# Mixture-of-experts block on one core: weight loads asked ahead in the dense stage, sliced table writes, and a fetch one chunk ahead in the second stage

## The chip, the cores and the metric

The kernel runs on one core of a Trainium2 chip. The metric is the time of one execution on the device in microseconds (us), taken as the median of several runs.

## The reference

The reference is one transformer block in fp32 on 512 tokens of width 2048: a mixer (attention and a recurrent unit, with modulated norms), then a layer of 16384 experts, then a final norm. The change touches the expert layer alone:

```python
q = (h @ w_q).reshape(B, S, 8, 2, 128)
s1 = einsum('bshd,hnd->bshn', q[..., 0, :], k1)     # 128 keys for each head
s2 = einsum('bshd,hnd->bshn', q[..., 1, :], k2)
v1, i1 = top_k(s1, 16);  v2, i2 = top_k(s2, 16)
vs, ic = top_k(v1[..., :, None] + v2[..., None, :], 16)   # best 16 of 256 sums
e = i1[ic // 16] * 128 + i2[ic % 16]                # 16 experts of 16384 a head
w = softmax(vs)
act = gelu(einsum('thkd,td->thk', u[e], h)) * w
y = einsum('thk,thkd->td', act, v[e])
```

Each token so has 128 chosen experts (8 heads, 16 each) out of 16384.

## The kernel before, in words

**How the work is split.** The 512 tokens are four tiles of 128. One tile is done by gathers: for each of its 128 choices, one row of u per token is gathered (L744), multiplied with the token and summed on DVE (L758), later one row of v is gathered and added on DVE (L756). This "side work" is sent in small portions between other work. The other three tiles (384 tokens) are done densely, in two stages.

**The dense stage** (about 1073 to 2370 us) multiplies all 16384 rows of u with the 384 tokens, as 128 blocks of 128 experts. `ublock` does a block in two halves. For each half `stream` loads 512 KB through SP's queue into `raw` (four buffers), and `hilo` splits it into two parts for precise fp32 products: a cast on ACT (L94) gives the high part, a subtraction on DVE (L95) the low part (three buffers each). Then come 24 matmuls (L690: eight column groups by three products). After each half, `pump` runs the list `todo`: 0.9 rows of side work, and one scatter of a list, if there is one. At the block's end ACT applies the gelu (L694, two buffers), and SP writes the result to two tables in memory: 128 KB to `tab2` (L696: two token tiles side by side) and 64 KB to `tab1` (L698: the third).

Between the blocks lie other pieces of work, traced in this order:
- Three decodes of the top choices (L611 to L640, on DVE), of which each ends in PE transposes (`rows`), with `ublocks(1)` to `ublocks(3)` after them. `ublocks(n)` does the blocks up to number n.
- Constants, and the zero fill of the tables' first rows and of two lists (DVE L811 and L815, writes of SP L812, L813, L817).
- `halves_of`, three times: for a token tile it builds the matrix of routing weights, 64 tokens at a time, so six "halves" in all. Sixteen steps of four tokens each make one-hot rows on DVE (L909, L914), multiply them on PE (L915, the "expansion matmuls", 768 in all) and copy the result on ACT into `ws` (L916, 4 MB, one buffer). The blocks are dealt out between the steps, 17 to a half. After the 16 steps, four writes of 1 MB go from `ws` to the table through SP's queue (L920, rows of 256 bytes), and four reductions of `ws` run on DVE (L921).
- `make_list`, twice: it picks out the rows of the table that any token uses (rounds of a maximum operation on DVE, a block after each fourth), scatters the list to memory (POOL, one to a `pump`) and reads it back (`done`, L890, on SP).
- The late top-k of the third tile: eight loads of scores (L934, `s12`, two buffers, SP), each followed by a search on DVE.

**The second stage** (about 2370 to 3104 us) goes through the listed rows in 171 chunks of 128 experts. `vchunk` gathers 128 rows of v (`gr`, L968 and what follows) and the rows of a table (`gw`), multiplies gelu and weight on DVE (L978), splits this into `gh` and `gl` (three buffers), splits the v rows in two halves (ACT L94, DVE L95), and multiplies on PE (L991), in the order gh with the high part, gh with the low part, gl with the high part. `vrun` calls `vchunk` for each chunk and then `step`, which sends the rest of the side work, and later the output's pieces. The first 76 chunks are 52 that serve two token tiles and 24 of the first tile alone; the other 95 serve one tile each and make up the stretch after about 2740 us.

**What orders the work.** The kernel is written in a language in which a planner orders each engine's instructions: program order is the priority, and an instruction whose inputs the planner expects later may be passed by a later one. `tc.keep_in_program_order(x)` takes this freedom away: x stays behind the instruction of the same engine that was traced before it. Each engine executes its own sequence in order, and a DMA is issued by one engine's queue (SP's, ACT's or POOL's) at its place in that sequence. An instruction that waits holds up all that stand behind it in that queue.

## Time and profile before

| | before |
|---|---|
| median of 3 runs | 3125.18 us (3118.3 to 3130.12) |
| the profiled execution | 3117.84 us, of which the span is 3116.0 us |
| busy PE | 2859.3 us (92%) |
| busy weight loads of PE | 2497.1 us (80%) |
| busy DVE | 2487.7 us (80%) |
| busy ACT | 1221.3 us (39%) |
| busy POOL | 928.6 us (30%) |
| bytes moved by DMA | 869.30 MB, mean 279 GB/s |
| mean granted clock of PE | 0.961 of full speed |

PE is TensorE, DVE is VectorE, ACT is ScalarE, POOL is GpSimd, SP is SyncE, which issues most of the loads and writes. "SPq" stands for SP's queue of DMA issues. A line of the profile names a line of the code (L690), the engine, the operation, and output<-input by the tiles' names; a number after x is a count; "<-" in a wait names what ended it. A matmul's weight load has rows of its own (PEld). The share of busy time over the whole span mixes three stages with different limits: the mixer and the projections up to 1073 us, the dense stage up to 2370 us, and the second stage up to 3104 us, with an end of 12 us behind it. The granted clock says at which share of its full speed PE was run.

### The profile page before, as it was taken

To read this page: it belongs to the slowest core of one execution; us is meant where nothing else is said; L and a number is where in the kernel's file an instruction comes from. 1 tells how busy PE (TensorE), PEld (TensorE's weight loads), DVE (VectorE), ACT (ScalarE), POOL (GpSimd) and SP (SyncE) were. 2 spreads that over 40 slices of the span, in tenths; PEclk is the share of its full clock that TensorE was granted. 3 is DMA by queue.
4 is the path that set the end of the run, shared out by engine and by line. 5 is a ranking of instruction groups with operands and counts; after the bars stand their busy time and mean duration, and the time that the engine had idled before them with its cause. 6 is when DMAs were issued, how large, how long until landed. Compare 5 with 4: busy or idle time off the path is not lost.

```text
span 3116.0 us, 39002 instructions
## 1 busy us (share of the span) xinstructions
PE 2859.3 (92%) x14093; PEld 2497.1 (80%) x14093; DVE 2487.7 (80%) x4100; ACT 1221.3 (39%) x1653; POOL 928.6 (30%) x673
## 2 busy tenths in 40 slices
PE   7899999989999999988899989998878999888887
PEld 5577777768788899988889989998877777766665
DVE  6877777873368898999988889999768888777777
ACT  5322223662232243333322223334223444555665
POOL 0000000000020002222223352422448777477774
PEclk9999999999999999999999999999989999999999
DMA  9767777333322368999999989999989999978885
GB/s 344 292 226 232 246 234 237 111 106 129 122 89 90 109 203 331 334 320 304 313 394 402 400 307 345 347 297 307 343 336 397 371 353 359 350 278 321 344 317 218
DMA packets 329502, 869.30 MB, mean 279 GB/s; under 512 B 125682, under 2 KB 181362, under 8 KB 274388
## 3 DMA queue, kind: packets, MB, share of 16 engines
q0 software_dynamic: 72512, 477.03, 40.5%
q1 hardware_dynamic: 256352, 389.52, 37.3%
q8 instruction: 112, 1.84, 0.2%
q14 instruction: 90, 0.74, 0.1%
q10 hardware_dynamic: 436, 0.18, 0.0%
HBM read 805.38 MB, written 61.25 MB: 278 GB/s over the span
## 4 chain that ended last, share of the span: by engine, by line
PE 56%; DVE 12%; DMA 10%; issue 7%; ACT 3%; POOL 2%; SPq 1%; another core or an unknown queue 0%; DVEq 0%; ACTq 0%; POOLq 0%
PE pj L690 25%; PE ps L991 11%; PE pj L660 6%; PE ps L526 4%; DMA araw<-w_ada 4%; DVE slo L95 4%; PE pj L302 3%; PE pj L991 2%; PE ps L915 2%; DVE gr L758 1%; DMA raw<-tab,igown 1%; PE pj L526 1%; DVE F L921 1%; ACT shi L94 1%; POOL gr L744 1%
## 5 line engine op out<-in xcount | busy, mean ns | idle before, releaser
L690 PE MATMUL pj<-dh,slo 128*128 128x384 f32 x2048 | 698.9, 343 | 53.7 <-DVE slo L95 53.5
L690 PE MATMUL pj<-dh,shi 128*128 128x384 f32 x2048 | 699.6, 342 | 21.1 <-ACT shi L94 21.1
L690 PE MATMUL pj<-dl,shi 128*128 128x384 f32 x2048 | 696.8, 340 | 0.0
L94 ACT CAST shi<-raw 128x1024 fp32r<-128x1024 f32 (+1 forms) x402 | 417.6, 1047 | 632.8 <-PE pj L690 243.5
L95 DVE TENSOR_TENSOR slo<-raw,shi 128x1024 fp32r<-128x1024 f32 (+1 forms) x402 | 487.7, 1217 | 217.1 <-ACT shi L94 196.3
L690 PEld LDWEIGHTS pj<-dh,slo 128*128 128x128 f32 x2048 | 392.4, 192 | 60.8 <-DVE slo L95 60.4
L95 DVE TENSOR_TENSOR slo<-gr,shi 128x1024 fp32r<-128x1024 f32 x342 | 405.6, 1222 | 41.4 <-ACT shi L94 34.6
L690 PEld LDWEIGHTS pj<-dh,shi 128*128 128x128 f32 x2048 | 393.3, 192 | 22.2 <-ACT shi L94 22.2
L690 PEld LDWEIGHTS pj<-dl,shi 128*128 128x128 f32 x2048 | 392.5, 192 | 0.1
L94 ACT CAST shi<-gr 128x1024 fp32r<-128x1024 f32 x342 | 342.1, 1046 | 107.6 <-PE ps L991 60.2
L744 POOL DMA_INDIRECT gr<-u_rows,ei x128 | 173.9, 1358 | 678.5 <-DVE gr L758 313.9
L756 DVE SCALAR_TENSOR_TENSOR y<-gr,dots,y 128x2048 f32<-128x2048 f32 x128 | 300.7, 2349 | 36.7 <-DMA gr<-v_rows,ei 36.4
L991 PE MATMUL ps<-shi,gh 128*128 128x512 f32 x740 | 254.0, 414 | 73.3 <-ACT gh L94 42.0
L148 DVE SCALAR_TENSOR_TENSOR araw<-araw,sil 128x1024 f32<-128x1024 f32 x192 | 233.8, 1222 | 104.8 <-DMA araw<-w_ada 101.9
L991 PE MATMUL ps<-slo,gh 128*128 128x512 f32 x740 | 297.4, 408 | 6.9 <-DVE slo L95 6.9
L758 DVE SCALAR_TENSOR_TENSOR gr<-gr,hrow 128x2048 f32<-128x2048 f32 x128 | 292.3, 2284 | 4.0 <-issue 4.0
L744 POOL DMA_INDIRECT gr<-v_rows,ei x128 | 198.3, 1549 | 311.4 <-DVE y L756 161.3
L991 PE MATMUL ps<-shi,gl 128*128 128x512 f32 x740 | 275.2, 399 | 1.6 <-DVE gl L95 1.6
L679 POOL CAST dh<-hh 128x384 fp32r<-128x384 f32 x16 | 10.4, 648 | 855.1 <-DVE hh L573 855.1
L991 PEld LDWEIGHTS ps<-shi,gh 128*128 128x128 f32 x740 | 143.9, 196 | 122.2 <-ACT gh L94 50.3
L694 ACT ACTIVATE ge<-pj 128x384 f32<-128x384 f32 x128 | 62.8, 490 | 422.4 <-PE pj L690 334.5
L302 PE MATMUL pj<-hh,shi 128*128 128x512 f32 x528 | 214.0, 405 | 6.6 <-ACT w L478 3.5
(353 smaller groups left out, 4996.2 us busy)
## 6 DMA issues: line engine op xcount, KB each, us to landing
raw<-peer_u SPq DMA_DIRECT2D x256, 512.0 KB
araw<-w_ada SPq DMA_DIRECT2D x192, 512.0 KB
raw<-w_in SPq DMA_DIRECT2D x66, 512.0 KB
tab<-ws SPq DMA_DIRECT2D x24, 1024.0 KB
raw<-w_out SPq DMA_DIRECT2D x32, 512.0 KB
raw<-w_q SPq DMA_DIRECT2D x32, 512.0 KB
tab<-ge SPq DMA_DIRECT2D x128, 128.0 KB
tab<-ge SPq DMA_DIRECT2D x128, 64.0 KB
```

The lines of the kernel that those rows point to most:

```text
L94: A.copy(hi, src)
L95: V.tensor_tensor(out=lo, in0=src, in1=hi, op=OP.subtract)
L148: V.scalar_tensor_tensor(out=r, in0=r, scalar=1.0, in1=sil[:, half * 1024:half * 1024 + 1024], op0=OP.mult, op1=OP.mult, accum_out=acc[:, ...
L302: PE.matmul(p, l[:, k8 * 128:k8 * 128 + 128], r, start=(k == 0 and i == 0), stop=(k == KC - 1 and i == 2))
L526: PE.matmul(po[t], l[:, ts], r[:, sl], start=(k == 0 and i == 0), stop=(k == KC - 1 and i == 2))
L660: PE.matmul(p, l[:, k8 * 128:k8 * 128 + 128], r, start=(k == 0 and i == 0), stop=(k == KC - 1 and i == 2))
L690: PE.matmul(p[:, :NDT], l[:, k8 * 128:k8 * 128 + 128], r, start=(k == 0 and i == 0), stop=(k == KC - 1 and i == 2))
L694: A.activation(ge, p[:, :NDT], AF.Gelu_apprx_tanh)
L744: return G.indirect_dma_start(out=out, out_offset=None, in_=src, in_offset=bass.IndirectOffsetOnAxis(ap=idx, axis=0))
L756: V.scalar_tensor_tensor(out=y0, in0=r, scalar=dots[:, j:j + 1], in1=y0, op0=OP.mult, op1=OP.add)
L758: V.scalar_tensor_tensor(out=r, in0=r, scalar=1.0, in1=hrow, op0=OP.mult, op1=OP.mult, accum_out=dots[:, j:j + 1])
L991: PE.matmul(banks[t][half * 2 + q2], l[:, ts], x[:, sl], start=first and i == 0, stop=end and i == 2)
```

## The change

It does five things:
- `uload` asks for the loads of u up to four halves ahead of their use, and keeps each in program order on SP. `ublock` takes the loaded tiles from a list.
- The two writes of a gelu result go through ACT's queue (`nc.scalar`).
- Each half's four writes of 1 MB become 32 slices of 128 KB, kept in program order on SP. They and the four reductions are put into a list, of which each `pump` takes five entries, ahead of the other work in `todo`. The blocks of a half are dealt out a little earlier, and the last of them follow after the slices were listed.
- `vchunk` is split in two: `vfetch` has the gathers, the product and the split into `gh` and `gl`; `vrun` calls it one chunk ahead.
- The order of the three products of the second stage becomes gh with the high part, gl with the high part, gh with the low part.

```diff
--- before.py
+++ after.py
@@ -680,10 +680,23 @@
             G.tensor_copy(dl[k], wl2[k][:, 128:])
     hps.close()
 
+    loads = []
+    asked = [0]
+
+    def uload(upto):
+        while asked[0] < min(upto, 2 * NB):
+            r = raw.tile([128, 1024], F32, name="raw")
+            tc.keep_in_program_order(nc.sync.dma_start(r, a["peer_u"][asked[0] // 2, asked[0] % 2]))
+            loads.append(r)
+            asked[0] += 1
+
     def ublock(b):
         p = pbank()
         for half in range(2):
-            uh, ul = stream(a["peer_u"][b, half])
+            uload(2 * b + half + 4)
+            uh = hl.tile([128, 1024], F32R, name="shi")
+            ul = hl.tile([128, 1024], F32R, name="slo")
+            hilo(uh, ul, loads.pop(0))
             for k8 in range(8):
                 k = half * 8 + k8
                 for i, (l, r) in enumerate(three(uh, ul, dh[k], dl[k])):
@@ -693,9 +706,9 @@
         ge = gq.tile([128, NDT], F32, name="ge")
         A.activation(ge, p[:, :NDT], AF.Gelu_apprx_tanh)
         rows = slice(128 + b * 128, 256 + b * 128)
-        nc.sync.dma_start(tab2[rows].rearrange("p (t x) -> p t x", t=2)[:, :, 0:128],
+        nc.scalar.dma_start(tab2[rows].rearrange("p (t x) -> p t x", t=2)[:, :, 0:128],
                           ge[:, 128:384].rearrange("p (t x) -> p t x", t=2))
-        nc.sync.dma_start(tab1[rows, 0:128], ge[:, 0:128])
+        nc.scalar.dma_start(tab1[rows, 0:128], ge[:, 0:128])
 
     dn = ExitStack()
     otp = pool(dn, "otp", side="right")
@@ -793,6 +806,14 @@
             if scatters:
                 scatters.pop(0)()
 
+    slices = []
+
+    def slices_some(n):
+        for _ in range(n):
+            if slices:
+                slices.pop(0)()
+
+    todo.append(lambda: slices_some(5))
     todo.append(lambda: side.send(GRATE))
     todo.append(lambda: scatter_some(1))
     for t in (1, 2):
@@ -902,7 +923,7 @@
             h0 = hf * TH
             ws = dz.tile([128, NB, TH], F32, name="ws")
             for t4 in range(TH // 4):
-                ublocks(lo + hf * step + t4 * (step - 3) // (TH // 4))
+                ublocks(lo + hf * step + t4 * (step - 5) // (TH // 4))
                 p = bank()
                 o1 = dz.tile([128, 4, 128], F32, name="o1", bufs=2)
                 t0 = h0 + t4 * 4
@@ -915,10 +936,19 @@
                     PE.matmul(p[:, j * 128:j * 128 + 128], o2, o1[:, j], start=True, stop=True)
                 A.copy(ws[:, :, t4 * 4:t4 * 4 + 4].rearrange("p i t -> p t i"), p.rearrange("p (t i) -> p t i", t=4))
             F = dz.tile([128, NB], F32, name="F", bufs=4)
-            for i in range(4):
-                sl = slice(i * 32, i * 32 + 32)
-                nc.sync.dma_start(tab[128 + i * 4096:4224 + i * 4096, c0 + h0:c0 + h0 + TH].rearrange("(i p) t -> p i t", p=128), ws[:, sl])
-                V.tensor_reduce(F[:, sl], ws[:, sl], axis=AX.X, op=OP.max)
+
+            def write(i, ws=ws, c=c0 + h0):
+                tc.keep_in_program_order(nc.sync.dma_start(
+                    tab[128 + i * 512:640 + i * 512, c:c + TH].rearrange("(i p) t -> p i t", p=128), ws[:, i * 4:i * 4 + 4]))
+
+            def most(i, ws=ws, F=F):
+                V.tensor_reduce(F[:, i * 32:i * 32 + 32], ws[:, i * 32:i * 32 + 32], axis=AX.X, op=OP.max)
+
+            for i in range(32):
+                slices.append(lambda i=i, w=write: w(i))
+                if i % 8 == 4:
+                    slices.append(lambda i=i // 8, m=most: m(i))
+            ublocks(lo + hf * step + step)
             Fs.append(F)
         V.tensor_tensor(out=Fs[0], in0=Fs[0], in1=Fs[1], op=OP.max)
         return Fs[0]
@@ -963,7 +993,7 @@
 
     halves = tab2.rearrange("r (h c) -> (r h) c", h=2)
 
-    def vchunk(ch, banks, flags, rows):
+    def vfetch(ch, rows):
         (idg, idv), c, top, ts_ = ch
         nt = len(ts_)
         w = nt * 128
@@ -977,6 +1007,11 @@
         g3 = gw.rearrange("p (t x) -> p t x", t=nt)
         V.tensor_tensor(out=g3[:, :, :128], in0=g3[:, :, :128], in1=g3[:, :, 128:], op=OP.mult)
         hilo(gh.rearrange("p (t x) -> p t x", t=nt), gl.rearrange("p (t x) -> p t x", t=nt), g3[:, :, :128])
+        return r, gh, gl
+
+    def vchunk(ch, got, banks, flags):
+        ts_ = ch[3]
+        r, gh, gl = got
         for half in range(2):
             pc = pieces(half)
             vh = pc.tile([128, 1024], F32R, name="shi")
@@ -987,7 +1022,7 @@
                 for j, t in enumerate(ts_):
                     first, end = flags[t]
                     ts = slice(j * 128, j * 128 + 128)
-                    for i, (l, x) in enumerate(((gh, vh), (gh, vl), (gl, vh))):
+                    for i, (l, x) in enumerate(((gh, vh), (gl, vh), (gh, vl))):
                         PE.matmul(banks[t][half * 2 + q2], l[:, ts], x[:, sl], start=first and i == 0, stop=end and i == 2)
 
     def main(n, more=False):
@@ -1012,12 +1047,15 @@
 
     def vrun(chunks, banks, both, step):
         where = {t: [i for i, ch in enumerate(chunks) if t in ch[3]] for t in range(3)}
+        ahead = []
         for i, ch in enumerate(chunks):
+            for k in range(i + len(ahead), min(i + 2, len(chunks))):
+                ahead.append(vfetch(chunks[k], gb if both(k) else vrp))
             flags = {t: (i == where[t][0], i == where[t][-1]) for t in ch[3]}
             for t in ch[3]:
                 if t not in banks:
                     banks[t] = four()
-            vchunk(ch, banks, flags, gb if both(i) else vrp)
+            vchunk(ch, ahead.pop(0), banks, flags)
             step(i)
 
     def mixed(xs, ys):
```

## Rows read from the trace of the kernel before

**Rows 1.** windows by stage: us, busy (x) per engine, PEclk, DMA share, GB/s

```profile
1073.00:2370.00 1297.00, 1203.52 (x6967) 1190.74 (x6966) 1155.50 (x1632) 429.05 (x508) 402.00 (x274) 0.96 0.93 329
1570.00:1780.00 210.00, 210.00 (x1206) 210.00 (x1206) 171.35 (x152) 61.23 (x76) 68.07 (x51) 0.99 1.02 404
2370.00:2740.00 370.00, 350.89 (x1476) 277.44 (x1475) 299.29 (x339) 173.38 (x228) 253.27 (x180) 0.98 0.95 363
2740.00:3104.00 364.00, 305.58 (x1195) 233.74 (x1193) 283.71 (x415) 221.75 (x308) 252.52 (x182) 0.94 0.81 303
```

**Rows 2.** waits of PE, 1073 to 2370: us in total, times, longest us

```profile
PE pj L690 <- DVE slo L95: 53.5, 18, 13.2
PE pj L690 <- ACT shi L94: 21.1, 5, 7.6
```

**Rows 3.** waits of SP's queue, 1190 to 2370

```profile
SPq L696 <- ACT ge L694: 358.8, 91, 8.4
```

**Rows 4.** timeline of SP at the end of the first half: start us, us, instruction

```profile
1302.24 17.63 SPq L920 DMA_DIRECT2D tab<-ws  x4
1319.97 7.29 SPq L99 DMA_DIRECT2D raw<-peer_u  x1
```

**Rows 5.** windows, sum of six, from 1300, 1380, 1460, 1540, 2090, 2160

```profile
sum 220.00, PE 167.76 PEld 160.52 DVE 195.32 ACT 63.76 POOL 35.92; mean PE 27.96 PEld 26.75 DVE 32.55 ACT 10.63 POOL 5.99
```

**Rows 6.** windows, sum of two, 1840 to 1870 and 2260 to 2300

```profile
sum 70.00, PE 43.16 PEld 41.88 DVE 40.20 ACT 9.70 POOL 34.86; mean PE 21.58 PEld 20.94 DVE 20.10 ACT 4.85 POOL 17.43
```

**Rows 7.** timeline of SP at the second list's read

```profile
2262.44 0.60 SPq L698 DMA_DIRECT2D tab<-ge  x1
2276.25 0.55 SPq L890 DMA_DIRECT2D sg<-list  x1
```

**Rows 8.** timeline of SP in the steady stretch

```profile
1588.05 0.53 SPq L696 DMA_DIRECT2D tab<-ge  x1
...
1596.42 0.52 SPq L696 DMA_DIRECT2D tab<-ge  x1
```

**Rows 9.** timeline of DVE, end of the third decode

```profile
1182.73 0.29 DVE L631 TENSOR_TENSOR se<-se,abf 128x128 f32<-128x128 f32 x1
...
1186.71 0.48 DVE L811 MEMSET pad<- 128x512 f32 x1
```

**Rows 10.** timeline of SP at the start of the dense stage

```profile
1071.26 0.38 SPq L722 DMA_DIRECT2D hrow<-hspill  x1
...
1188.31 0.88 SPq L817 DMA_DIRECT2D list<-padi  x2
```

**Rows 11.** timeline of POOL at the start of the dense stage

```profile
1180.34 0.13 POOL L808 IOTA pm<- 128x1 f32 x1 [48.86 <-DVE se L628]
```

**Rows 12.** groups of DVE, 1085 to 1187: xcount, busy us, mean ns, idle before

```profile
L95 DVE TENSOR_TENSOR slo<-raw,shi 128x1024 fp32r<-128x1024 f32 x25 | 30.4, 1219 | 4.9 <-ACT shi L94 4.9
```

**Rows 13.** timeline of SP at the late top-k

```profile
1808.51 1.24 SPq L934 DMA_DIRECT2D s<-sspill  x2
```

**Rows 14.** timeline of DVE at the late top-k

```profile
1808.61 0.28 DVE L831 TENSOR_SCALAR ig<-lf,pm 128x128 int32<-128x128 f32 x1
```

**Rows 15.** groups of DVE, 1800 to 1905

```profile
L589 DVE FIND_INDEX8 i<-v,s 128x8 uint32<-128x128 f32 x14 | 3.9, 285 | 0.0
...
L588 DVE MAX8 vs<-cd 128x8 f32<-128x256 f32 x6 | 2.5, 418 | 0.0
```

**Rows 16.** waits of PE, 2740 to 3104

```profile
PE ps L991 <- ACT gh L94: 42.0, 19, 5.1
```

**Rows 17.** timeline of DVE in the second stage

```profile
2900.38 6.94 DVE L95 TENSOR_TENSOR slo<-gr,shi 128x1024 fp32r<-128x1024 f32 x6 [0.26 <-issue]
2907.25 0.48 DVE L978 TENSOR_TENSOR raw<-raw 128x128 f32<-128x128 f32 x2
```

**Rows 18.** timeline of PE in the second stage

```profile
2907.91 0.50 PE L991 MATMUL ps<-shi,gh 128*128 128x512 f32 x1 [1.68 <-ACT gh L94]
```

**Rows 19.** waits of PE, 2370 to 2740

```profile
PE ps L991 <- ACT shi L94: 18.5, 12, 6.5
```

## The prediction

> **What bounds the kernel now.** I read the busy time by stage first. The dense stage, from 1073 to 2370 us, is 1297 us, of which PE is busy for 1203.5 us and idle for 93.5 us at a mean granted clock of 0.96 [rows 1]. One stretch of it, 1570 to 1780, shows what the stage could be: PE busy all 210 us, with DMA at its full share [rows 1]. There a half block (24 matmuls) takes 4.18 us, 1206 matmuls in 210 us, so 128 blocks need 1070 us. What is left of 1203.5 is for the 768 expansion matmuls, and for matmuls at the lower clock level. The second stage, 2370 to 3104, is 351 + 306 us of PE work and 77 us of idle time; its second part, one token tile to a chunk, is idle for 58 us of 364 [rows 1].
>
> Next, who PE waits for. In the dense stage it is the casts and differences of the weight parts (53.5 and 21.1 us) [rows 2]. Behind them lies SP's queue, which keeps its order: SP stands in front of the writes of the gelu results for 358.8 us in all, until ACT has the gelu [rows 3], and the loads that stand behind such a write wait with it. At the end of each half of the scatter-matrix work, SP is held for 17.6 us by four writes of 1 MB, and the next load takes 7.3 us more to issue [rows 4]; DVE does four reductions in a row there. The stretches around the six ends have 220 us with 167.8 us of PE work, so 52.2 us idle [rows 5]. Two others, where SP waits to read a list back before it goes on with loads, have 43.2 us of PE work in 70 us, 26.8 us idle [rows 6]: SP does nothing from 2263.0 to 2276.3 us there [rows 7].
>
> **The change, part by part.**
>
> Small writes to ACT's queue: 128 pairs leave SP, where a pair is a block apart and the first takes 0.53 us [rows 8]. ACT issues them instead, about 1.1 us more for each block of 8.36 us, in which it now has 3.4 us of work (429 us over 128 blocks [rows 1]). ACT is three parts ahead of PE; I cost this at nothing. Without that cover it would be 128 x 1.1 = 141 us. SP no longer waits for a gelu, which is the gain that the next item counts. The Trainium skill, "DMA: Bandwidth & Descriptors" (Issuing engines are not separate DMA queues), says that issuing from several engines saves only the sequencer's time for the issue. By that alone the item is worth nothing here; the row on SP's wait says that the order in the queue, not the issue, was the cost.
>
> The big writes in 32 slices, the reductions one by one, five items to a half block: 36 items take 7.2 half blocks, six times over. The 52.2 us go, but the slices ask for the same bytes within some 30 us, beside a load and 0.9 row gathers per half block, when the DMA share is already 1.02 in the steady stretch [rows 1]. Bounds: 0 (the four parts loaded ahead, 4 x 4.18 us, hide it all) and 52 us (as now). I take 18, 3 us an end, since the load now stands behind only five slices instead of four whole writes.
>
> List reads: 26.8 us now. The scatters still go one to a half block, and loads stand three half blocks ahead. I take 5 (bounds 0 and 27).
>
> Loads kept in program order: this is the part that can cost. Each load is now pinned behind the SP instruction traced before it, whatever that waits for. At the start, loads 0 to 8 are traced before the four zero-fill writes of the tables and lists; load 9 and all others stand behind them. The zero fill is written by DVE at 1186.7 us, after the last step of the third decode [rows 9], and SP issues its last writes at 1188.3 [rows 10]; until now the loads passed them. That such a thing holds up what is pinned behind it, the trace shows on POOL: its gathers wait 48.9 us for a constant in the same state [rows 11]. After the change DVE has less beside the three decodes: of the 25 differences (30.4 us) that it did between 1085 and 1187 [rows 12] only some six are left, so 22 us less, and some 5 us of waits go. The zero fill then comes near 1160, a load follows at 1162, is cast and subtracted by 1167. PE also starts late: the first loads now stand behind a read that SP issues at 1071.3 [rows 10], so PE begins near 1078 instead of 1073. It has nine half blocks, 38 us, with some matmuls of the stage before between them, until about 1119. So some 48 us of waiting and 5 us of late start: 53 us. Bounds: 0 if the fill gets memory earlier than now, 80 if the decodes go no faster.
>
> The same at the late top-k: the half loads from 151 on stand behind the last of eight reads of scores, which has two buffers, so it waits until six heads are through on DVE. In the trace the reads begin at 1808.5 us, just as DVE makes the first list's rows [rows 13, 14]. A head is ten operations of 0.28 us and six of 0.42 [rows 15], 5.3 us; six are 32 us, some 41 us with differences between. The fixed order of the list's rounds behind the blocks puts PE four parts behind, 17 us. So 24 us; bounds 0 and 41.
>
> Dense sum, idle time: 53 + 24 + 18 + 5 and 14.5 that I leave as it is (93.5 - 52.2 - 26.8) is 114.5 against 93.5, +21 us. Fewer, longer gaps let fewer matmuls run at the lower clock: 1203.5 less 1070 and about 90 for the 768 expansion matmuls and small work leaves some 43 us lost now; I take 27, -16. Together **+5 us: the dense stage gives nothing back in sum.**
>
> Second stage: in its second part PE waits 42.0 us for the cast of the gated rows [rows 16]. DVE puts the product of two gathered tiles behind six differences in a row, 6.9 us, until 2907.3 [rows 17], and PE stands 1.7 us until 2907.9 for its cast [rows 18]. With the fetch of a chunk traced ahead of the work of the one before, product and casts come first in the order, and the change of the matmuls' order asks for the second difference last. I take two thirds of the 42, 28 us, and a third of the 22 us that the clock of 0.94 over 364 us costs [rows 1], 7 us: -35. Bounds: +10 (a product waits on DVE for its gather with differences queued behind it) and -64 (58 idle and some clock; DVE has 284 us of work there, under the 300 that would leave). The waits for the weight casts in the first part, 18.5 us [rows 19], stay.
>
> **Sum:** +5 - 35 = -30 us on the profiled execution's 3117.8, 3088 us; the median of the runs is 7.3 us above that execution, so **3095 us**.
>
> **Rivals.**
>
> The pins hold nothing up (chance 0.18): the zero fill and the score reads find their memory earlier. For it: no program-order reason ties the fill to the decodes. Against: the fill follows the last decode step at once, while differences of later blocks ran before it [rows 9, 12]. Then the dense stage loses 37.5 us instead of 93.5 and 16 us of slow clock: -72 - 35, 3018 us.
>
> Slices too slow (0.20), the one that ends slower: from where five slices and a load keep SP over 4.18 us, a slice over 0.77 us. By rows, an eighth of a big write is 17.63 / 32 = 0.55 us [rows 4]; by its rows of data it has twice those of a small write of 0.53 us [rows 8], 1.06. At 1.06 SP lacks 1.45 us in each of 43 half blocks, 63 us in place of 18, and 10 us more at the low clock: 3150 us. For it: transfers already fill the DMA share. Against: 0.55 comes from the same transfer. The Trainium skill, "DMA: Bandwidth & Descriptors" (Bandwidth), has it that one should batch to 1 MiB or more, with 341 GB/s measured at 1 MB and 138 at 64 KB. By that, as an estimate, 25 MB of slices take up to 182 us instead of 74, and the change would end near 3185 us. The trace does not show it for a queue that is kept full.
>
> The order was not the cause in the second stage (0.20): the gathers themselves are late, as 0.81 of the DMA share [rows 1] makes possible, and DVE only passes it on. Then -35 goes and 3130 us is left.
>
> The forecast as worked out: 0.42.
>
> **How the numbers follow.** A measurement here can tell about 0.5%, 15.6 us. The forecast's own range is 3060 to 3135, and most of it is faster: 0.36, with 0.05 within 0.5% and 0.01 slower. The first rival adds 0.18 to faster; the second 0.20 to slower; the third 0.16 to the same and 0.04 to slower. So faster 0.54, same 0.21, slower 0.25. The range takes in the forecast, the first rival and most of the second: 3020 to 3165.
>
> **What would show it.** In the new profile: a gap of PE of some 45 us before 1170, closed by the first load after the zero fill; a second of some 20 us with SP standing before a read of scores; SP no longer waiting for the gelu; the six ends without a gap over 5 us; expansion matmuls spread over the blocks instead of bunched; PE's wait for the gated cast under 20 us after 2740. Wrong: no gap at the start (first rival), SP busy all through the slices (second), or the wait for the gated cast as long as now (third).

## The result, and the profile after

The changed kernel takes 3280.4 us (median of 6 runs) beside 3121.7 us of the kernel before: a ratio of 1.051 (95% interval 1.049 to 1.053). It is slower by 5%, where the forecast was faster by 1%. One of the six runs was in a slow state (7149 us) and is left out of the ratio. The profiled execution has a span of 3277.6 us beside 3116.0.

The stages first (busy time by stage; columns as in [rows 1], which these three lines answer). The stages' borders have moved: the last dense matmul is at 2530 us now.

```profile
1073.00:2530.00 1457.00, 1217.27 (x6951) 1194.26 (x6950) 1173.08 (x1634) 429.23 (x500) 413.85 (x275) 0.91 0.85 298
2530.00:2900.00 370.00, 344.32 (x1458) 274.21 (x1457) 279.46 (x328) 174.50 (x231) 234.01 (x175) 0.98 0.91 343
2900.00:3265.00 365.00, 314.72 (x1237) 238.67 (x1235) 288.30 (x425) 225.83 (x315) 247.71 (x186) 0.94 0.82 310
```

The whole loss lies in the dense stage: 1457 us in place of 1297. PE is idle for 239.7 us there (93.5 before), and its busy time grew by 14 us as well, with a granted clock of 0.91 in place of 0.96: after a long gap the first matmul of a half block takes 0.69 us, where one takes 0.33 in the steady stretches. From the last dense matmul to the last one of the chunks it is 734 us, 747 before.

Where the idle time lies, by stretches of the dense stage (same columns):

```profile
1119.00:1185.00 66.00, 12.31 (x53) 9.72 (x52) 56.46 (x70) 7.38 (x9) 14.34 (x14) 0.57 0.55 212
1910.00:1990.00 80.00, 47.48 (x236) 45.50 (x236) 80.00 (x185) 12.75 (x15) 17.09 (x18) 0.77 0.89 319
1990.00:2062.00 72.00, 19.10 (x97) 17.21 (x96) 72.00 (x78) 8.29 (x10) 40.62 (x20) 0.63 0.84 309
...
1460.00:1510.00 50.00, 37.38 (x193) 35.91 (x191) 28.60 (x31) 7.96 (x10) 11.27 (x9) 0.86 1.05 336
1650.00:1700.00 50.00, 33.29 (x155) 31.20 (x154) 21.80 (x20) 6.65 (x9) 8.48 (x7) 0.80 1.05 329
```

Three kinds of places can be told apart.

**The start.** PE is idle for 53.7 of the 66 us from 1119 on. PE's timeline has the gaps, SP's timeline the load that ends them:

```profile
1130.32 0.45 PE L745 MATMUL ps<-ident,se 128*128 128x128 f32 x1 [8.80 <-DVE se L628]
...
1144.58 0.48 PE L745 MATMUL ps<-ident,se 128*128 128x128 f32 x1 [13.81 <-DVE se L631]
...
1172.24 2.90 PE L936 MATMUL ps<-o,o 128*128 128x128 f32 x12 [11.53 <-DVE o L935]
...
1180.70 0.69 PE L703 MATMUL pj<-dh,shi 128*128 128x384 f32 x1 [2.08 <-ACT shi L94]
```

```profile
1081.67 14.05 SPq L689 DMA_DIRECT2D raw<-peer_u  x5
1160.81 0.33 SPq L833 DMA_DIRECT2D tab<-pad  x1
...
1163.64 1.43 SPq L689 DMA_DIRECT2D raw<-peer_u  x3
```

After nine half blocks PE goes straight to the transposes of the decodes (L745), which wait for DVE. The tenth load follows the zero fill at 1163.6 us, as the prediction had it (1162). That the fill is not what costs the time, the runs will show.

**The late top-k.** From 1910 to 2062 us PE is idle for 85.4 us. The first part is the one that was forecast: SP stands at the score reads for 31.8 us with the loads behind it. The second part was not: PE stands at the transposes of the late decode again.

```profile
1927.05 31.83 SPq L964 DMA_DIRECT2D s<-sspill  x4
```

```profile
1967.08 0.69 PE L703 MATMUL pj<-dh,shi 128*128 128x384 f32 x1 [23.48 <-ACT shi L94]
...
2025.61 0.45 PE L745 MATMUL ps<-ident,se 128*128 128x128 f32 x1 [26.22 <-DVE se L628]
...
2046.23 0.48 PE L745 MATMUL ps<-ident,se 128*128 128x128 f32 x1 [20.18 <-DVE se L631]
```

**The six ends.** Five of the six ends with slices lose 62.0 us of PE time together (the stretches from 1280, 1460, 1650, 1840 and 2160; 14.5, 12.6, 16.7, 8.0 and 10.2), and three later places lose 4.2, 7.1 and 5.6 us where the four reductions still run in a row on DVE. Before, the ends lost 52.2 [rows 5]. At the second end SP puts slices between the loads, and ACT's timeline shows who else stands:

```profile
1476.43 8.03 SPq L689 DMA_DIRECT2D raw<-peer_u  x1
1484.51 4.29 SPq L941 DMA_DIRECT2D tab<-ws  x4
...
1489.69 3.72 SPq L941 DMA_DIRECT2D tab<-ws  x5
```

```profile
1475.21 0.49 ACT L707 ACTIVATE ge<-pj 128x384 f32<-128x384 f32 x1 [0.38 <-PE pj L703]
1489.80 0.52 ACTq L709 DMA_DIRECT2D tab<-ge  x1
...
1491.13 1.04 ACT L94 CAST shi<-raw 128x1024 fp32r<-128x1024 f32 x1 [15.43 <-DMA tab<-ws]
```

The gelu is ready at 1475.7, but ACT's write of it goes out at 1489.8, and the cast that PE needs stands behind that write on ACT. Such waits, from the end of ACT's instruction before a write to the write, sum up to 133 us over the 256 small writes, 123 of it in 24 waits while slices go out.

The sixth end is different. From 2320 to 2352 us all 32 slices go out and PE does not lose anything, while POOL issues no gather (busy times of that stretch and of the second end):

```profile
2320.00:2352.00 32.00, 32.00 (x187) 32.00 (x186) 26.14 (x61) 8.69 (x11) 0.00 (x0) 1.00 1.06 260
1480.00:1512.00 32.00, 19.38 (x88) 17.91 (x87) 10.22 (x9) 4.59 (x6) 3.56 (x3) 0.79 1.04 307
```

### The profile page after: what moved, and what is told of

It reads as the page before. It is cut to its first block, busy times and chain, and to the rows that moved or that the text cites. A ratio compares the mean times of both kernels' runs of the same rounds, so it can differ in the third digit from the quotient of the medians.

```text
span 3277.6 us, 39134 instructions
## 1 busy us (share of the span) xinstructions
PE 2876.4 (88%) x14093; PEld 2502.7 (76%) x14093; DVE 2487.8 (76%) x4100; ACT 1224.3 (37%) x1652; POOL 916.3 (28%) x673
## 5 line engine op out<-in xcount | busy, mean ns | idle before, releaser
L757 POOL DMA_INDIRECT gr<-u_rows,ei x128 | 208.4, 1628 | 644.1 <-DVE gr L771 297.9
L1026 PE MATMUL ps<-shi,gh 128*128 128x512 f32 x740 | 270.3, 411 | 62.5 <-ACT gh L94 37.9
L1026 PE MATMUL ps<-shi,gl 128*128 128x512 f32 x740 | 298.8, 407 | 9.0 <-DVE gl L95 8.5
L771 DVE SCALAR_TENSOR_TENSOR gr<-gr,hrow 128x2048 f32<-128x2048 f32 x128 | 291.1, 2282 | 12.6 <-DMA gr<-u_rows,ei 12.4
L1026 PE MATMUL ps<-slo,gh 128*128 128x512 f32 x740 | 266.2, 402 | 2.3 <-DVE slo L95 2.3
L757 POOL DMA_INDIRECT gr<-v_rows,ei x128 | 179.5, 1402 | 278.8 <-DVE y L769 142.8
L302 PE MATMUL pj<-hlo,shi 128*128 128x512 f32 x528 | 213.2, 404 | 0.0
```

What stands on the lines that cost most here:

```text
L302: PE.matmul(p, l[:, k8 * 128:k8 * 128 + 128], r, start=(k == 0 and i == 0), stop=(k == KC - 1 and i == 2))
L757: return G.indirect_dma_start(out=out, out_offset=None, in_=src, in_offset=bass.IndirectOffsetOnAxis(ap=idx, axis=0))
L771: V.scalar_tensor_tensor(out=r, in0=r, scalar=1.0, in1=hrow, op0=OP.mult, op1=OP.mult, accum_out=dots[:, j:j + 1])
L1026: PE.matmul(banks[t][half * 2 + q2], l[:, ts], x[:, sl], start=first and i == 0, stop=end and i == 2)
```

## The experiments

| run | edit | median, us | ratio to before (95%) |
|---|---|---|---|
| changed kernel | | 3280.4 | 1.051 (1.049 to 1.053) |
| e2_fill | zero fill ahead of the decodes | 3282.8 | 1.054 (1.052 to 1.057) |
| e3_s12 | eight buffers for score reads | 3272.4 | 1.051 (1.048 to 1.054) |
| i2_two_pins | 2 of 256 pins left | 3271.3 | 1.047 (1.037 to 1.057) |
| i1_load_order | loads pinned to each other alone | 3186.6 | 1.020 (1.011 to 1.029) |
| e4_unpin | no load pinned | 3182.0 | 1.022 (1.019 to 1.025) |
| f1_ge_sp | e4, small writes on SP | 3172.7 | 1.018 (1.014 to 1.021) |
| h3_wide | f1, 3 entries a half block | 3165.2 | 1.016 (1.006 to 1.026) |
| g2_half | f1, 8 pieces of 512 KB | 3163.2 | 1.015 (1.011 to 1.019) |
| g1_mb | f1, 4 pieces of 1 MB | 3144.2 | 1.008 (1.005 to 1.010) |
| f3_big | e4, four writes of 1 MB at once | 3115.5 | 0.999 (0.997 to 1.000) |
| g3_big_sp | f3, small writes on SP | 3108.6 | 0.996 (0.995 to 0.998) |
| g4_pins | f3 with the pins | 3244.2 | 1.040 (1.037 to 1.043) |
| f2_ge_act | before, small writes on ACT | 3139.4 | 1.006 (1.003 to 1.009) |
| e1_second | before, second stage's part | 3106.1 | 0.997 (0.995 to 0.998) |
| f4_two | e1, two chunks ahead | 3108.0 | 0.996 (0.994 to 0.999) |
| h1_slow_slices | f1, 0.5 gathers a half block | 3250.4 | 1.043 (1.034 to 1.053) |
| h2_slow_big | g3, 0.5 gathers a half block | 3277.2 | 1.052 (1.042 to 1.062) |

Each ratio is to runs of the kernel before that were taken together with the run. The h and i runs were executed twice each, the others 4 to 12 times.

### What holds PE at the start and at the late top-k

The prediction named two holders on SP: the zero fill, and the score reads that wait for a buffer. Another was possible. What `keep_in_program_order` takes as "the instruction before" on SP need not be a DMA: where a memory pool is closed and another opened, the memory is handed over, and the planner expects that when the memory's last user is done. Behind the ninth load (load 8) the decodes' memory goes over to the pools `lp1` and `dz`; between load 156 and load 157 that of the late top-k goes over to `dz2`, and SP issues nothing else between these two. A load that is pinned there comes late in the planner's order, and with it the cast, the difference and the matmuls that use it. The hand-over is read from the program, and no trace shows it on SP. What the traces show is the order that came out of it: PE has 216 dense matmuls (9 x 24) ahead of the second decode's transposes, and 3768 (157 x 24) ahead of the late decode's. In the kernel before these counts are 376 and 4298.

The zero fill moved ahead, e2_fill:

```diff
+    with tc.tile_pool(name="tp1", bufs=1, reuse_waits="tile") as tp1:
+        pad = tp1.tile([128, 256], F32, name="pad")
+        V.memset(pad, 0.0)
+        nc.sync.dma_start(tab2[:128, :256], pad)
...
     se, wv = decode(tp, tts[0])
```

> The changed kernel with the zero fill of tables and lists written ahead of the first decode, so that no load stands behind it. Fill theory (the prediction's): the gap of PE between 1119 and 1185 us, 53 us of idle time, goes, and the time is 3225 us. Boundary theory: load 9 is pinned behind more than DMAs, namely behind the point where the memory of the third decode is handed to the next pool (pools lp1 and dz); that point waits for the decodes as well, so the gap stays and the time stays at 3280 us.

More buffers, e3_s12:

```diff
-            s12 = tp0.tile([128, 2, 128], F32, name="s12", bufs=2)
+            s12 = tp0.tile([128, 2, 128], F32, name="s12", bufs=8)
```

> The changed kernel with eight buffers in place of two for the eight score reads of the late top-k, so that no load waits for a read. Read theory (the prediction's): the loads behind the reads come 30 us earlier, the idle 86 us between 1910 and 2062 shrink to some 20, and the time is 3215 us. Boundary theory: 157 half blocks still stand ahead of the point where the late top-k's memory is handed on, which waits for its decode; PE then waits the same time in one gap in place of two, and the time is 3265 to 3280 us.

Both left the time where it was. In e2_fill the fill goes out before the first load, and SP has nothing but loads from 1072 us on. Loads 9 to 12 are issued from 1096 us on and are not held. PE still stops at the decodes' transposes after nine half blocks, and ACT's cast for the tenth comes only behind the copy of the last decode's transposes, at 1155.6 us (SP's timeline, then PE's, then ACT's):

```profile
1069.98 0.88 SPq L758 DMA_DIRECT2D list<-padi  x2
...
1072.33 126.90 SPq L689 DMA_DIRECT2D raw<-peer_u  x20
```

```profile
1096.08 11.19 SPq L689 DMA_DIRECT2D raw<-peer_u  x4
```

```profile
1138.99 0.47 PE L745 MATMUL ps<-ident,se 128*128 128x128 f32 x1 [13.68 <-DVE se L631]
```

```profile
1155.21 0.48 ACT L746 COPY oT<-ps 128x384 f32<-128x384 f32 x1 [13.08 <-PE ps L745]
1155.59 1.05 ACT L94 CAST shi<-raw 128x1024 fp32r<-128x1024 f32 x1
```

So it is not the late load but the order of PE and ACT that holds the work. The fill has a part in the gap: from 1085 to 1200 us PE is idle for 36.5 us, against 53.7. But the stage as a whole is not shorter, as other places lose more.

At the late top-k it is the same. In the changed kernel load 157 is issued at 1978.9 us, and its cast follows at 2052.4, behind the late decode (SP's timeline, then ACT's):

```profile
1978.88 80.47 SPq L689 DMA_DIRECT2D raw<-peer_u  x5
```

```profile
2046.96 0.48 ACT L746 COPY oT<-ps 128x384 f32<-128x384 f32 x1 [40.00 <-PE ps L745]
...
2052.38 2.01 ACT L94 CAST shi<-raw 128x1024 fp32r<-128x1024 f32 x2
```

In e3_s12 all score reads are out by 1891 us, the gap of 23.5 us is gone, and the wait at the decode has grown to 54.2 us from 26.2 (PE's timeline):

```profile
2019.52 0.45 PE L745 MATMUL ps<-ident,se 128*128 128x128 f32 x1 [54.16 <-DVE se L628]
...
2040.14 0.47 PE L745 MATMUL ps<-ident,se 128*128 128x128 f32 x1 [20.17 <-DVE se L631]
```

Then no pins, e4_unpin:

```diff
-            tc.keep_in_program_order(nc.sync.dma_start(r, a["peer_u"][asked[0] // 2, asked[0] % 2]))
+            nc.sync.dma_start(r, a["peer_u"][asked[0] // 2, asked[0] % 2])
```

> The changed kernel with the loads of u not kept in program order, everything else as it is. Pin theory: the idle 57 us at the start and 86 us around the late top-k go, less some 15 us that the kernel before had there too, and about 10 us of slow clock: 3140 us; the six ends with slices keep their idle time (75 us) and the reductions in a row theirs (17). Rival (slices and full DMA queues are the cause, the pins only show it): 3230 us or more, and new gaps in place of the two that go.

98 us come back, where 140 were expected: the ends lose more now, some 87 us in gaps of over 1.5 us (below). The last two runs of this set show the place itself. One pins each load to the load before it alone; the other keeps the pins of load 9 and load 157 alone:

```diff
+            if last:
+                tc.add_manual_dep(ld.ins, last[-1].ins.name, ...)
+            last.append(ld)
```

```diff
+            if asked[0] in (9, 157):
+                tc.keep_in_program_order(ld)
```

> The changed kernel with each load kept behind the load before it and behind nothing else. Boundary theory: a fixed order of the loads among themselves costs nothing, 3182 us like the kernel without pins, no gap at the start and none around the late top-k. Rival (any fixed order of 256 loads takes from the planner what it needs): 3250 us or more.

> The changed kernel with two of the 256 pins left, at load 9 and load 157, the first that are traced behind a hand-over of the decodes' memory. Boundary theory: both gaps are back in full, PE stops after 9 and after 157 half blocks, 3265 to 3285 us. Rival (the loss comes from the many pins together): 3182 to 3200 us.

Two pins of 256 bring back all that the pins cost, to within the noise; a fixed order of the loads among themselves costs nothing (i1 and e4 are not apart). Pinned to load 156, load 157 does no harm; pinned to whatever is traced before it, it does. PE's counts say the same: 216 and 3768 in i2, 376 and 4416 in i1. The same stretch, 1119 to 1185 us, in the run with loads pinned to each other and in that with two pins:

```profile
1119.00:1185.00 66.00, 65.17 (x376) 64.42 (x375) 60.15 (x58) 22.84 (x28) 8.62 (x8) 1.00 0.62 212
```

```profile
1119.00:1185.00 66.00, 10.85 (x36) 7.79 (x36) 56.44 (x65) 4.69 (x7) 14.29 (x13) 0.50 0.51 200
```

### What the slices and ACT's queue cost

e4_unpin still loses 66 us to the kernel before. At its first end SP issues all 32 slices in one go (SP's timeline), and ACT stands at a small write for 20.1 us of it, from the gelu's end at 1315.8 us on (ACT's timeline):

```profile
1297.97 37.51 SPq L941 DMA_DIRECT2D tab<-ws  x32
```

```profile
1315.34 0.49 ACT L707 ACTIVATE ge<-pj 128x384 f32<-128x384 f32 x1 [3.35 <-PE pj L703]
1335.93 0.53 ACTq L709 DMA_DIRECT2D tab<-ge  x1
```

So two theories stood: ACT's own writes, or the slices. Three runs tell them apart: the small writes back on SP (f1_ge_sp), the small writes on ACT with nothing else changed (f2_ge_act), and four large writes with the small ones still on ACT (f3_big):

```diff
-        nc.scalar.dma_start(tab1[rows, 0:128], ge[:, 0:128])
+        nc.sync.dma_start(tab1[rows, 0:128], ge[:, 0:128])
```

```diff
-            for i in range(32):
-                slices.append(lambda i=i, w=write: w(i))
...
+            for i in range(4):
+                sl = slice(i * 32, i * 32 + 32)
+                nc.sync.dma_start(tab[128 + i * 4096:4224 + i * 4096, ...], ws[:, sl])
+                V.tensor_reduce(F[:, sl], ws[:, sl], axis=AX.X, op=OP.max)
```

> The kernel with unpinned loads, and the small writes of the gelu back on SP's queue; slices stay. In the run with unpinned loads ACT stood 160 us in front of its own small writes, in pieces of 2 to 24 us, all while slices were issued. ACT theory (a DMA that ACT issues waits while the queues are full of slices, and the casts behind it on ACT wait with it): without them some 75 us of the dense stage come back, 3105 us. Slice theory (32 small writes are slow by themselves, the loads behind them come late): the gaps at the six ends stay, 3170 to 3185 us.

> The kernel before, with the small writes on ACT's queue and nothing else. ACT theory: ACT stands in front of them during the four writes of 1 MB at each of the six ends, 10 to 17 us each and 60 us or more in all, and the time is 3150 us or more. Rival (the prediction's: a move at no cost, and SP, which stood 359 us in front of these writes, is free for the loads): 3090 to 3122 us.

> The kernel with unpinned loads, with four writes of 1 MB and four reductions at once in place of the 32 slices; small writes stay on ACT's queue. ACT theory: the same bytes fill the queues, ACT stands as long, 3165 to 3195 us. Slice theory: the loss at the six ends falls back to the 52 us of the kernel before, 3120 us.

The slices cost most. With large writes the loss is gone (3115.5), with ACT relieved and slices kept it is nearly all there (3172.7; e4 and f1 are not clearly apart). ACT's queue alone costs 0.6% (0.3 to 0.9) on the kernel before, 17 us, where the prediction had nothing. ACT stands at its writes for 169 us in e4_unpin, but for 39 in f3_big, so it is the slices that make it stand. What this costs beside the slices is small: with the writes back on SP it is 9 us less (f1), and beside large writes 7 us less (g3), neither clear of the noise. In f1 ACT is held in another way at the first end: its next copy into the one buffer `ws` stands ahead of the casts and waits until the slices have landed (ACT's timeline):

```profile
1349.03 1.89 ACT L937 COPY ws<-ps 128x512 f32<-128x512 f32 x2 [20.08 <-DMA tab<-ws]
```

One part is not split off: the 192 slices are pinned in program order as well, and the large writes of f3_big are not. No run has slices without pins. Against the pins as the cause stands that the changed kernel's sixth end has pinned slices and loses nothing.

The pins with large writes (g4_pins) and the best of these parts (g3_big_sp):

> The changed kernel with four writes of 1 MB at once in place of the 32 slices; loads kept in program order, small writes on ACT's queue. If pins and slices add: the 98 us of the pins on top of 3115.5, 3214 us. If the pins cost so much only because slices stand in the same fixed order: 3150 us or less.

> As the kernel with unpinned loads and four writes of 1 MB at once (3115.5 us), with the small writes of the gelu on SP again. By the run that moved only these writes to ACT (17 us slower than before): 3098 to 3106 us. Rival (with large table writes ACT loses only 39 us in front of its writes, and SP's wait for the gelu costs as much): 3115 us, no change.

The pins cost 129 us without the slices, more than the 98 beside them, so the two losses overlap. g3_big_sp beats both kernels, by 0.4% against the one before, but no more than its second stage's part does alone (e1_second, below); it and f3_big are too close to tell apart.

Size and spread, from f1_ge_sp with the number of pieces, and of entries to a half block, changed (g1_mb; g2_half has eight pieces and three entries):

```diff
-    todo.append(lambda: slices_some(5))
+    todo.append(lambda: slices_some(2))
-            for i in range(32):
+            for i in range(4):
```

> As the kernel with unpinned loads and the small writes on SP, with the table writes in four pieces of 1 MB in place of 32 slices of 128 KB; still from the list, one write and one reduction to a half block, writes kept in program order. Size theory (32 DMAs of 128 KB take SP twice as long as four of 1 MB, 32 to 38 us against 16 to 18 in each end, and hold the loads and the buffer of the matrix that long): 3110 us or less beside 3173 with slices. Spread theory (what is late is that the writes are strewn between the loads and the next half's copies wait longer for the buffer): 3140 us or more.

> The same with eight pieces of 512 KB, three entries of the list to a half block. Size theory: between the runs with 4 pieces and with 32, near the one with 4: 3110 to 3125 us. Spread theory: 3150 us, like the run with 32.

Neither theory alone: 4, 8 and 32 pieces take 3144, 3163 and 3173 us (8 and 32 are not clearly apart), so size has a part, but even four pieces of 1 MB cost 36 us more when they are dealt out one by one, and pinned, than when they go at once. Little of that lies at the ends: from 5 us before an end's first write to 20 us behind its last, g1 is idle for 58.8 us in all and g3 for 52.5. Where the rest comes from was not followed up. What most of them share is a DMA share of about 1 at the ends. So the last question was whether the queues have room at all. Fewer gathers give room; a thinner spread only helps if the rate was the trouble:

```diff
-GRATE = 0.9
+GRATE = 0.5
```

> The kernel with unpinned loads, small writes on SP and 32 slices (3173 us), with 0.5 row gathers to a half block in place of 0.9; what is not gathered by the end of the dense stage is gathered in the second stage, which gets longer for it, so the dense stage alone is compared (first to last dense matmul, 1336 us with 0.9). Queue theory (the DMA queues are full in the steady stretch, share 1.02, so 4 MB more at each end cost their own time): with the gathers cut the queues have room, the idle time of PE in the six ends falls below 25 us, and the dense stage is within 15 us of the one with four large writes at 0.5. Small-DMA theory (32 issues hold SP by themselves): the dense stage stays some 60 us longer than with large writes.

> The partner: unpinned loads, small writes on SP, four writes of 1 MB at once, 0.5 row gathers to a half block (dense stage 1275 us with 0.9). Queue theory: the six ends lose little here too, dense stage 1220 to 1250 us. Small-DMA theory: the same as with 0.9 at the ends, 1260 to 1275 us.

> The kernel with unpinned loads, small writes on SP and 32 slices, three entries of the list to a half block in place of five, so that an end's slices take 12 half blocks in place of 7. Rate theory (five slices and a load are too much for one half block): 3140 us or less beside 3173. Queue theory (the queues have no room in any half block, the same bytes cost the same time however thin they are spread): 3160 to 3185 us.

With 0.5 gathers to a half block the order turns round. First to last dense matmul it is 1336 us (slices) against 1275 (large) at 0.9, and 1231 against 1251 at 0.5 (one profile each). The busy time summed over the six ends, in this order: slices at 0.9, large at 0.9, slices at 0.5, large at 0.5 (f1, g3, h1, h2):

```profile
sum 314.00, PE 238.93 PEld 229.21 DVE 224.32 ACT 66.38 POOL 60.68; mean PE 39.82 PEld 38.20 DVE 37.39 ACT 11.06 POOL 10.11
```

```profile
sum 232.00, PE 184.60 PEld 178.72 DVE 210.73 ACT 59.05 POOL 42.69; mean PE 30.77 PEld 29.79 DVE 35.12 ACT 9.84 POOL 7.12
```

```profile
sum 246.00, PE 225.67 PEld 222.34 DVE 181.42 ACT 72.30 POOL 20.81; mean PE 37.61 PEld 37.06 DVE 30.24 ACT 12.05 POOL 3.47
```

```profile
sum 202.00, PE 166.59 PEld 161.25 DVE 179.44 ACT 53.49 POOL 21.76; mean PE 27.77 PEld 26.88 DVE 29.91 ACT 8.92 POOL 3.63
```

Sum less PE is the idle time: 75.1, 47.4, 20.3 and 35.4 us. So 28 of the 61 us between f1 and g3 are idle time at the ends; some 18 are idle time elsewhere, and for some 15 PE is busy longer. In h1 the first two ends, which still have gathers beside them, make all of the 20.3; the other four have none, and lose nothing. One of those four, from 1560 to 1600 us:

```profile
1560.00:1600.00 40.00, 40.00 (x233) 40.00 (x232) 17.60 (x17) 12.42 (x15) 0.00 (x0) 1.00 1.04 279
```

In h2 only the last two ends are free of gathers, and lose 2.4 us together. An end beside gathers loses 10.2 us on average in h1 and 8.3 in h2. So the turn need not mean that slices win: four of h1's ends happen to fall where no gather runs, and only two of h2's.

The traces show why the gathers matter. In e4_unpin, where SP is held by single slices for up to 3.7 us at the first end, the gathers' packets (the queue `software_dynamic`) take the DMA engines nearly alone from 1322 to 1324 us; from 1308 to 1310, with no gather in flight, SP's packets (`hardware_dynamic`) have them, and a slice holds SP for 0.5 us (DMA view of the two windows, in this order: packets, MB, share of the 16 engines):

```profile
q0 software_dynamic: 67, 0.55, 93.6%
q1 hardware_dynamic: 2, 0.00, 0.1%
```

```profile
q1 hardware_dynamic: 1683, 0.42, 93.0%
```

Over all 192 slices of that run, 42 of the 43 that held SP for over 1.5 us did so while gathers moved over 5% of the bytes.

The three entries of h3_wide changed nothing that can be told from f1, but at three of its ends (1302, 2132 and 2226 us) SP still issued all 32 slices in a row, so only the other three were dealt out more thinly. So the queue theory holds in this form: beside gathers the slices find the engines taken and cost time, with no gain from dealing them out more thinly where that took effect; without gathers PE loses nothing by them. The DMA share does not tell the two apart: it is 1.06 and 1.04 at ends that lose nothing. The runs at 0.5 are slower in all because the gathers left over stretch the second stage (929 and 938 us in place of some 735).

### The second stage by itself

```diff
+            for k in range(i + len(ahead), min(i + 2, len(chunks))):
+                ahead.append(vfetch(chunks[k], gb if both(k) else vrp))
```

In f4_two, i + 3 stands in place of i + 2.

> The kernel before with the second stage's part of the change alone (fetch one chunk ahead, order of the three products). By the traces the second stage (last dense matmul to last chunk matmul) went from 746.9 to 733.8 us, 13 less. If the two parts of the change don't touch each other: 3109 us beside 3122 before (ratio 0.996). If the gain comes only from a different state of the side work at the end of the dense stage: no change, 3122. If the forecast's 35 us was right and the dense part took some of it back: 3087.

> The kernel before with the second stage's part, fetching two chunks ahead in place of one. Order theory (the product of the gathered rows still comes late in DVE's order): PE's wait for the cast of the gated rows falls from 38 to under 20 us, 3090 us beside 3106 with one chunk ahead. Rival (DVE's own work and the gathers set the pace, with buffers for three chunks only): no change, 3100 to 3112 us.

The part is worth 0.3% (0.2 to 0.5), some 10 us, and a second chunk ahead adds nothing. PE's wait for the gated rows' cast is 37.9 us in the changed kernel's last stretch (2900 to 3265) and 39.3 with two chunks ahead (2740 to 3102), against 42.0 [rows 16]:

```profile
PE ps L1026 <- ACT gh L94: 37.9, 25, 8.8
```

```profile
PE ps L996 <- ACT gh L94: 39.3, 23, 9.3
```

DVE's timeline of the changed kernel shows the product behind three differences in one place, where [rows 17] had it behind six in another. Over the last stretch 16 of 93 products stood behind five or more differences in a row before, and 1 of 96 does now:

```profile
3209.26 3.64 DVE L95 TENSOR_TENSOR slo<-gr,shi 128x1024 fp32r<-128x1024 f32 x3
3212.81 0.28 DVE L1008 TENSOR_TENSOR raw<-raw 128x128 f32<-128x128 f32 x1
```

## Why the prediction was wrong

**The start: 53 us, right size by luck.** Measured are 53.7 us of idle time from 1119 on and a first dense matmul 6.7 us later than before. The step that failed is "load 9 and all others stand behind" the zero fill: it looked for what SP waits for, and left out that a pin moves the order of PE and ACT as well. Load 9 does come behind the fill, at 1163.6 us, but in e2_fill loads 9 to 12 were out from 1096 us on, 36.5 us of the gap stayed, and the time did not fall.

**The late top-k: 24 forecast, 85 measured.** The step was "the half loads from 151 on stand behind the last of eight reads". That is 32 us of it. The rest was missed: PE and ACT have the late decode ahead of half block 157, whose load was out at 1978.9 us, and DVE, busy for 72 of 72 us there, puts 19 of the side work's sums of 2.34 us among the decode's steps. The upper bound of 41 us knew only the reads. Without their wait (e3_s12) PE stands as long in one place.

**The slices: 18 forecast, 62 at five ends and 17 at bunched reductions measured.** The step that failed is "0 ... and 52 us (as now)" as bounds. That the change could make the ends worse was left to a rival, although [rows 1] had the DMA share at 1.02, gathers included, in the stretch that was to take up the slices. The rival's mechanism (a slice takes up to 1.06 us) was right: 0.53 us each at the sixth end without gathers (5 in 2.66), 1.17 with them (32 in 37.51). The Trainium skill, "DMA: Bandwidth & Descriptors" (Bandwidth), says that one should batch to 1 MiB or more. Beside the gathers the runs agree (3144 us with 4 pieces, 3173 with 32); at the ends without gathers slices lose nothing and large writes 2.4 us.

**The small writes: "I cost this at nothing".** On the kernel before they cost 17 us. The step left out that a write on ACT can wait. ACT's three parts of lead cover an issue of 1.1 us, not the stands of 14 to 24 us beside slices; why f2_ge_act loses 17 us with none over 9.0 us is open. The Trainium skill, "DMA: Bandwidth & Descriptors" (Issuing engines are not separate DMA queues), says that DMAs of several engines run on the same 16 engines and that a second issuing engine saves only the issue. f2_ge_act agrees in so far as nothing was gained.

**The list reads: 5 forecast, 12.5 measured** (2400 to 2440 us). **The slow clock: 16 us fewer forecast, 14 more measured.** The step "Fewer, longer gaps" failed: PE's gaps of over 1.5 us in the dense stage became longer (216 us in all, 75 before) but not fewer (28, and 16 before).

**The second stage: 35 forecast, 13 measured.** The step "I take two thirds of the 42" held the order in the program for the order on DVE. The order on DVE did change, with 1 product in place of 16 behind five or more differences, and the wait only fell to 38 us. The third rival was right that the order bought little; the gathers as its reason were not tested alone. A sign for them: DVE still waits 23.0 us for a gathered table ahead of the product in that stretch (26.8 before).

**The sum.** The idle time named here comes to 230 of the 239.7 us. The pins were one of the rivals' questions and the slices another, each with its own chance, as if only one could go wrong. Both did, and 98 (pins), some 9 (ACT's queue beside slices, not clearly above nothing) and 64 us (slices, f1 against g3) less 11 (what is left gains on the kernel before) are the 160 us by which the kernel is slower, taken away in that order. The range ended at 3165.

## What to carry to other kernels

Before an instruction is pinned in program order, list everything that is traced ahead of it on its engine, hand-overs of memory included, and ask when the planner expects the last of these to be done: the order of the other engines follows from that, even if the load itself is issued early. Pin loads to each other, or not at all. Before transfers are moved or cut up, look at what else moves in the stretch that is to take them up: here the gathers decided what they cost, and the DMA share alone did not tell. An engine that feeds the critical one should not issue DMAs that can wait for those of another.

## What was not expected of the hardware

ACT's write waited for a DMA of SP, although the two come from different engines. The trace's semaphore records tell for which. The DMAs of SP and ACT share eight semaphores, the counters that tell of a landing, and a write on ACT waits until the last DMA with its own semaphore has landed. The write at 1335.93 us in e4_unpin waits for semaphore 108, which the slice issued at 1323.79 raises for the last time at 1335.85. All 21 stands of over 1.5 us in that run end within 0.5 us behind such a landing: 15 of a slice, 4 of a load and 2 of ACT's own writes. So ACT does not wait for the end of SP's run of slices (a pair of its writes goes out amid it, at 1309.6), but for one landing, which here came 12.1 us behind the slice's issue.

And a DMA can hold the engine that issues it: while gathers move, single slices hold SP for up to 3.7 us at that end, in place of 0.5. At which point of the DMA's path the slice is stopped can't be told from these runs.
